# One half of the differential v moved a stage later, and the head norms moved forward, in a decoder block with two attention branches

## The chip, the cores and the metric

The kernel runs on one core of a Trainium2 chip. The core has five engines that work side by side, each with its own queue in a fixed order: TensorE (PE, matmuls and transposes, with weight loads shown as PEld), VectorE (DVE), ScalarE (ACT), GpSimd (POOL) and SyncE (SP), which here issues nearly all loads. Results of matmuls land in PSUM, from where DVE or ACT must move them before the PSUM tile can be used again. The metric is the device time of one launch in microseconds (us); less is better.

## What is computed

The block works on 512 tokens of 1024 channels in float32. Cut to what matters:

```python
xn = rmsnorm(x, norm_mix_g)
q_lat, kv_lat, k_rope, dq, dk, dv, gate_pre = split(xn @ w_in)
# branch A, MLA: 8 heads; q and k from low-rank latents plus a rotary part
o_mla = causal_attention(q_mla, k_mla, v_mla)
# branch B, differential attention: 4 heads, each with two score maps and v of 128 columns
o1 = causal_attention(dq[..., 0, :], dk[..., 0, :], dv)
o2 = causal_attention(dq[..., 1, :], dk[..., 1, :], dv)
o_diff = rmsnorm(o1 - lam * o2, diff_subln_g) * (1 - lambda_init)
gates = sigmoid(gate_pre + b_gate)                     # 2 x 1024 channels
x = x + (g_mla * (o_mla @ w_branch_mla) + g_diff * (o_diff @ w_branch_diff)) @ w_out
x = x + (silu(hn @ w_ffn_gate) * (hn @ w_ffn_up)) @ w_ffn_down     # hn = rmsnorm(x)
return rmsnorm(x, norm_final_g)
```

Causal means that a query block of 128 tokens looks at itself and the blocks before it.

## The kernel before

**Precision.** Every float32 operand of a projection is kept as a pair of rounded halves, high and low (`split`, line 242; `weights`, line 267, for what is loaded), and each product is three matmuls: high by high, high by low, low by high (`mm3`, lines 298 to 300). For a loaded weight tile the high half is made on ACT (L260) and the low half on DVE (L265), 1024 elements a row.

**Tiles.** Buffers come from pools with a fixed number of tiles for each tag (`BUFS`, line 39): 22 "L" tiles of 1024 words a row (q, k, v, pairs of gates, outputs of heads), 5 "t" temporaries of 512, 4 "raw" and 3 "w" tiles for loaded weights and their halves, 6 "P" for probabilities. In PSUM there are 3 "mm" tiles for projections, 2 "sc" for scores, 2 "tr" for transposes and the norm's sums, 1 "pv" for values.

**Order.** The program is traced once, and a scheduler then sets the order of each engine's queue by priorities and its own picture of time: a lower number goes first among what is ready. Three classes are used (lines 124 to 141). `feed` (from 1000 on) is ahead of all: roundings of weights that are used whole, the first two steps of a rotation (L557, L558) and the draining of gates (L480). `attention`, entered with `urgent()`, starts at 100000: the heads. All else has the number of its place in the program, from 1000000 on: this is the fill, projections that are to keep PE busy while a head waits for its softmax.

**Stages.** The fill lists (lines 46 to 54) say which projection is traced ahead of which head. `FILL_MLA` has one entry for each of the four pairs of MLA heads, `FILL_DIFF` one for each differential head. Their items are: `mqk` (q and k of a pair of MLA heads), `mr` (their rotary rows, copied by DMA), `pe` and `mv` (rotary part and v of MLA), `qk` h (q and k of a differential head), `v` c (v of the differential heads 2c and 2c + 1), `gate` b, m (gate of branch b, channels 128m on). A gate, and each of q and k, is 24 matmuls of 512 columns into one "mm" tile with one loaded weight tile. A `v` is 96 matmuls of 256 columns into two "mm" tiles with two loaded weight tiles. Two neighbouring gates (m even and m + 1) share one "L" tile; the even one asks for it (lines 476 to 478). Each half of `v` is drained by four splits into an "L" tile of its own (lines 601 to 605), and q and k of a head take three "L" tiles (line 580) after a rotation in two "t" tiles each (line 555).

**A differential head** (`diff_head`, line 673): for each of four query blocks two maps of scores (L626), on DVE the masked copy with the row maximum (L630), on ACT the exponential (L158), on DVE the reciprocal (L633), then both maps joined (L679 on ACT, L680 on DVE). Then P is transposed on PE (L652) and split (L245, L249), multiplied with v (L663), and the result is copied to a "t" tile (L686) and squared into another (L687). The squares are split into an "L" tile (L690 on DVE, L691 on POOL).

**The norm of a head** (`diff_norm`, line 694): two matmuls with ones sum the squares over the channels into a "tr" tile (L698), then Ln and Exp on ACT, three steps on DVE (L702, L703, L705), one on POOL (L704), and a split into an "L" tile of its own (line 706; L247 on ACT, L251 on DVE). In the loop over the heads (lines 811 to 819) the norm of head h − 1 is traced inside the fill of head h, behind the first item of its list and at the fill's priority; that of the last head is urgent.

After the heads come the 16 sigmoids, the MLA branch (line 825), the differential branch, the output projection, and the FFN.

Of the kernel before, what the change touches and what calls it, by code (L numbers as in the profile page):

```python
# [2 lines left out]

# [1 line left out]

# [16 lines left out]
P = 128  # L22
S = 512
D = 1024
KD = D // P
# [10 lines left out]
OFF = (0, 512, 896, 1152)  # L36
MAGIC = 12582912.0
TWO_PI = 6.283185
BUFS = dict(X=2, L=22, P=6, PT=1, raw=4, w=3, t=5, sm=24)
LAST = 256  # L40
N_WARM = 10
P_DVE = (0, 1)
# [2 lines left out]
W_ENG_BRANCH = ['dve', 'dve']  # L45
FILL = [[("pe", 0), ("mr", 0), ("gate", 0, 2), ("mv", 0)]]
FILL_MLA = [[("mqk", 1), ("mr", 1), ("v", 0), ("pe", 1)],
            [("mqk", 2), ("mr", 2), ("v", 1), ("mv", 1)],
            [("mqk", 3), ("mr", 3), ("qk", 0)],
            [("qk", 1)]]  # L50
FILL_DIFF = [[("qk", 2), ("gate", 0, 3)],
             [("qk", 3), ("gate", 0, 4), ("gate", 0, 5)],
             [("gate", 0, 6), ("gate", 0, 7), ("gate", 1, 0)],
             [("gate", 1, m) for m in range(1, KD)]]
PBUFS = dict(mm=3, sc=2, tr=2, pv=1)


# [31 lines left out]
def build(ctx, nc, tc, a, out):  # L89
# [5 lines left out]
    def nm(s):  # L95
        uid[0] += 1
        return f"{s}_{uid[0]}"

    def T(tag, shape, dtype):
        return sb.tile(shape, dtype, name=nm(tag), tag=tag, bufs=BUFS[tag])  # L100

# [3 lines left out]
    def L_():  # L105
        return T("L", [P, 2, S], F32R)
# [4 lines left out]
    def tmp():  # L111
        return T("t", [P, S], F32)
# [7 lines left out]
    def dma(o, i):  # L120
        nc.sync.dma_start(out=o, in_=i)
# [14 lines left out]
            tc.cur_priority = self.saved  # L136

    attention, feed = Ahead(100000), Ahead(1000)

    def urgent():  # L140
        return attention
# [115 lines left out]
    def round_hi(o, i):  # L257
        if w_eng[0] == 'act':
            with tc.issue_after(hi_last.ins):
                nc.scalar.activation(out=o, in_=i, func=AF.Copy)  # L260
        else:
            nc.vector.tensor_copy(out=o, in_=i)
# [4 lines left out]
    def weights(src, n0, n1, pick=None):  # L267


        raw = T("raw", [P, 1024], F32)  # L270
        n = n0 * n1
        rv = raw[:, :n].rearrange("p (a b) -> p a b", a=n0)
        if isinstance(src, list):
            for i, s_ in enumerate(src):
                dma(rv[:, i, :].rearrange("p (h d) -> p h d", h=s_.shape[1]), s_)
        else:
            dma(rv, src)
        w = T("w", [P, 2, 1024], F32R)
        if pick is None:
            with feed:  # L280
                round_hi(w[:, 0, :n], raw[:, :n])
                round_lo(w[:, 1, :n], raw[:, :n], w[:, 0, :n])
        else:
            nk = sum(h * (d1 - d0) for h, d0, d1 in pick)
            wv = [w[:, s, :n0 * nk].rearrange("p (a b) -> p a b", a=n0) for s in range(2)]
            c = 0
            for h, d0, d1 in pick:
                src_ = rv.rearrange("p a (h e) -> p a h e", h=h)[:, :, :, d0:d1]
                hi, lo = [v[:, :, c:c + h * (d1 - d0)].rearrange("p a (h e) -> p a h e", h=h) for v in wv]
                c += h * (d1 - d0)  # L290
                round_hi(hi, src_)
                round_lo(lo, src_, hi)
            n = n0 * nk
        return [w[:, i, :n].rearrange("p (a b) -> p a b", a=n0) for i in range(2)]
# [196 lines left out]
    qk = {}  # L491

    def fill(work):
        for kind, *args in work:
            if kind == "gate":
                gate(*args)
            elif kind == "v":
                diff_v(*args)
            elif kind == "qk":
                qk[args[0]] = diff_qk(*args)  # L500
            elif kind == "pe":
                pe[args[0]] = mla_pe(*args)
            elif kind == "mv":
                mv[args[0]] = mla_v(*args)
            elif kind == "mqk":
                mqk[args[0]] = mla_qk(*args)
            elif kind == "mr":
                mla_rope(args[0], mqk[args[0]], pe[args[0] // 2])
# [164 lines left out]
    def diff_head(h, products):  # L673
        blocks = []
        for i, p1 in enumerate(prob_tiles()):
            p2 = T("P", [P, S], F32)[:, :(i + 1) * P]
            r1, r2 = scores(list(zip(products, (p1, p2))), i)
            nc.vector.tensor_mul(out=r2, in0=r2, in1=neg_lam)
            nc.scalar.activation(out=p2, in_=p2, func=AF.Copy, scale=r2)  # L679
            nc.vector.scalar_tensor_tensor(out=p1, in0=p1, scalar=r1, in1=p2, op0=ALU.mult, op1=ALU.add)  # L680
            blocks.append(p1)
        pt = transposed(blocks)
        ps = values(pt, lambda j, s: dv[(h // 2) * 2 + j // 2][:, s, (j % 2) * 256 + (h % 2) * P:
                                                              (j % 2) * 256 + (h % 2) * P + P])
        o32, sq = tmp(), tmp()
        nc.scalar.activation(out=o32, in_=ps, func=AF.Copy)  # L686
        nc.scalar.activation(out=sq, in_=ps, func=AF.Square)  # L687
        sqs = L_()
        sqs = [sqs[:, 0, :], sqs[:, 1, :]]
        nc.vector.tensor_copy(out=sqs[0], in_=sq)  # L690
        nc.gpsimd.tensor_sub(out=sqs[1], in0=sq, in1=r32(sqs[0]))  # L691
        return o32, sqs

    def diff_norm(o32, sqs):

        ps = PS("tr")
        for s in range(2):
            nc.tensor.matmul(out=ps, lhsT=ones_r, rhs=sqs[s], start=s == 0, stop=s == 1)  # L698
        y, u = tmp(), tmp()
        log_exp(out=y, in_=ps, func=AF.Ln, scale=1.0 / P, bias=eps)  # L700
        last_exp[0] = log_exp(out=y, in_=y, func=AF.Exp, scale=-0.5)
        nc.vector.scalar_tensor_tensor(out=u, in0=ps, scalar=P * EPS, in1=y, op0=ALU.add, op1=ALU.mult)  # L702
        nc.vector.scalar_tensor_tensor(out=u, in0=u, scalar=-0.5 / P, in1=y, op0=ALU.mult, op1=ALU.mult)  # L703
        nc.gpsimd.tensor_mul(out=o32, in0=o32, in1=y)  # L704
        nc.vector.scalar_tensor_tensor(out=u, in0=u, scalar=1.5, in1=o32, op0=ALU.add, op1=ALU.mult)  # L705
        o = L_()
        split(u, o[:, 0, :], o[:, 1, :], col(R_SG))
        return o

# [85 lines left out]
    mqk, pe, mv = {}, {}, {}  # L795
# [5 lines left out]
    for p in range(4):  # L801
        o = L_()
# [6 lines left out]

    o_diff, parts = [], []  # L810
    for h in range(4):
        fill(FILL_DIFF[h][:1])
        if h > 0:
            o_diff.append(diff_norm(*parts[h - 1]))
        fill(FILL_DIFF[h][1:])
        with urgent():
            parts.append(diff_head(h, qk[h]))
    with urgent():
        o_diff.append(diff_norm(*parts[3]))
# [19 lines left out]
    for c in range(8):  # L839
        half, kp = c // 4, c % 4  # L840
        raw = T("raw", [P, 1024], F32)
        dma(raw.rearrange("p (a b) -> p a b", a=2), kview("w_out", half * S, S, 2 * kp, 2))
        w = None
        if c < 3:
            w = T("w", [P, 2, 1024], F32R)
        elif c == 3:
            w = T("PT", [P, 2, 1280], F32R)
# [36 lines left out]
    for f, n in products[:3]:  # L884
        w = weights(kview(n, f * P, P), KD, P)
# [5 lines left out]
    for n_, (f, n) in enumerate(products):  # L891
        if n_ < 3:
            ps, w = early[n_]
            ffn_product(ps, w, 256, 512)
        else:
            w = weights(kview(n, f * P, P), KD, P)
# [50 lines left out]
    for half in range(2):  # L947
# [8 lines left out]
        for k0 in range(0, NF, 2):  # L956
            w = weights(kview("w_ffn_down", half * S, S, k0, 2), 2, S)
# [42 lines left out]
```

## Time and profile before

| | |
|---|---|
| median of 3 runs | 749.19 us (749.06 to 750.64) |
| the profiled execution | 749.08 us, of it the span of the profile 747.3 us |
| MLA heads, first score matmul to the first differential one | about 74 to 159 us |
| differential heads, first score matmul to the last value matmul | about 159 to 278 us |
| MLA branch begins | 289 us |

The profile is one execution taken by the hardware profiler; times in it run from the start of its span. PE's matmuls are pipelined and their ends are modelled, so PE's busy time holds some overlap; a window in which it is below its full length has real idle time. The views that are used are the page (busy times, the chain that ended last), the windows (busy time and count of each engine in a stretch, also for one line alone), the timeline (instructions in order, with the idle time ahead of them and what ended it in brackets) and groups by line.

### The profile page before, as it was taken

What the parts mean: (1) busy time and instruction counts of PE and PEld (TensorE: products, weight loads), DVE (VectorE), ACT (ScalarE), POOL (GpSimd) and SP (SyncE); (2) the same over time, 40 slices, a digit from 0 to 9 for tenths busy, and PEclk for the clock granted to TensorE, in tenths of its full rate; (3) what the DMA queues carried; (4) which work ended last, traced back from release to release, by engine and by line L of the source; (5) the groups of instructions that cost most, each with busy time, mean ns of one, the idle gap of its engine ahead of it and who ended that gap; (6) DMA issues with size and microseconds to landing.
All of it is one profiled execution on the core that took longest, in us unless ns stands there. A gap on an engine that the chain in (4) does not pass through costs nothing.

```text
span 747.3 us, 9538 instructions
## 1 busy us (share of the span) xinstructions
PE 731.1 (98%) x3602; PEld 618.2 (83%) x3602; DVE 416.9 (56%) x812; ACT 332.5 (44%) x613; POOL 49.9 (7%) x45
## 2 busy tenths in 40 slices
PE   9998999999989989999999999999999999999996
PEld 7977999888868878888898888888888888888885
DVE  7787798988897765695544333342333332122424
ACT  7764788767665633643414232222323222122314
POOL 1000000321240101000000000000000000000302
PEclk9999999999999999999999999999999999999999
DMA  9615344523432312339114333323233232323202
GB/s 336 197 50 137 102 116 100 134 65 97 113 85 63 107 57 85 113 114 281 29 56 114 99 98 89 110 84 113 84 102 96 87 110 86 112 86 109 89 1 112
DMA packets 100414, 78.82 MB, mean 105 GB/s; under 512 B 6416, under 2 KB 87056, under 8 KB 100368
## 3 DMA queue, kind: packets, MB, share of 16 engines
q1 hardware_dynamic: 100080, 78.13, 35.5%
q8 instruction: 28, 0.46, 0.3%
q14 instruction: 18, 0.15, 0.1%
q10 hardware_dynamic: 288, 0.08, 0.0%
HBM read 71.91 MB, written 2.10 MB: 99 GB/s over the span
## 4 chain that ended last, share of the span: by engine, by line
PE 68%; DVE 6%; ACT 2%; issue 1%; DMA 0%; DVEq 0%; ACTq 0%
PE ps_mm L298 19%; PE ps_mm L299 19%; PE ps_mm L300 19%; DVE w L265 2%; PE ps_sc L298 1%; PE ps_sc L300 1%; PE ps_tr L300 1%; PE ps_tr L298 1%; PE ps_tr L299 1%; PE ps_sc L299 1%; DVE P L630 1%; PE ps_pv L300 1%; PE ps_pv L298 1%; PE ps_pv L299 1%; DVE L L249 1%
## 5 line engine op out<-in xcount | busy, mean ns | idle before, releaser
L265 DVE TENSOR_TENSOR w<-raw,w 128x1024 fp32r<-128x1024 f32 (+3 forms) x114 | 136.1, 1196 | 160.7 <-ACT w L260 160.0
L260 ACT ACTIVATE w<-raw 128x1024 fp32r<-128x1024 f32 (+3 forms) x110 | 109.5, 998 | 254.3 <-issue 154.6
L298 PE MATMUL ps_mm<-X,w 128*128 128x512 f32 (+1 forms) x568 | 217.8, 384 | 4.7 <-DVE t L558 4.6
L299 PE MATMUL ps_mm<-X,w 128*128 128x512 f32 (+1 forms) x568 | 217.7, 383 | 0.0
L300 PE MATMUL ps_mm<-X,w 128*128 128x512 f32 (+1 forms) x568 | 217.3, 383 | 0.0
L298 PEld LDWEIGHTS ps_mm<-X,w 128*128 128x128 f32 x568 | 107.1, 189 | 26.0 <-issue 2.8
L299 PEld LDWEIGHTS ps_mm<-X,w 128*128 128x128 f32 x568 | 107.3, 189 | 20.0 <-issue 0.2
L300 PEld LDWEIGHTS ps_mm<-X,w 128*128 128x128 f32 x568 | 107.2, 189 | 20.0
L905 DVE TENSOR_TENSOR t<-t,ps_mm 128x512 f32<-128x512 f32 x22 | 15.1, 688 | 66.4 <-PE ps_mm L300 65.7
L158 ACT ACTIVATE P<-P,sm 128x128 f32<-128x128 f32 (+3 forms) x64 | 35.7, 558 | 25.6 <-DVE sm L630 25.2
L931 POOL TENSOR_TENSOR L<-L,P 128x512 f32<-128x512 f32 (+1 forms) x9 | 12.6, 1414 | 436.2 <-ACT t L930 436.2
L626 PE MATMUL ps_sc<-L,L 96*128 96x128 f32 (+7 forms) x160 | 36.6, 324 | 1.2 <-DVE sm L630 1.2
L299 PE MATMUL ps_mm<-w,L 128*128 128x512 f32 (+1 forms) x100 | 37.2, 372 | 0.0
L298 PE MATMUL ps_mm<-w,L 128*128 128x512 f32 (+1 forms) x100 | 37.1, 373 | 0.0
L300 PE MATMUL ps_mm<-w,L 128*128 128x512 f32 (+1 forms) x100 | 37.0, 373 | 0.0
L299 PE MATMUL ps_mm<-L,w 128*128 128x512 f32 x90 | 35.4, 394 | 0.0
L298 PE MATMUL ps_mm<-L,w 128*128 128x512 f32 x90 | 35.2, 393 | 0.0
L300 PE MATMUL ps_mm<-L,w 128*128 128x512 f32 x90 | 35.2, 391 | 0.0
L245 ACT ACTIVATE L<-t 64x512 fp32r<-64x512 f32 (+2 forms) x47 | 29.2, 621 | 10.2 <-DVE t L779 3.7
L630 DVE CUSTOM_DVE_ANT_0 P<-ps_sc,mask 128x128 f32<-128x128 f32 (+3 forms) x64 | 30.6, 477 | 3.5 <-PE ps_sc L626 3.3
L626 PEld LDWEIGHTS ps_sc<-L,L 96*128 96x128 f32 (+1 forms) x160 | 27.1, 189 | 4.9 <-DVE sm L630 1.7
L249 DVE TENSOR_TENSOR L<-t,L 128x512 fp32r<-128x512 f32 (+2 forms) x37 | 27.7, 749 | 3.6 <-ACT L L245 3.1
(271 smaller groups left out, 1136.6 us busy)
## 6 DMA issues: line engine op xcount, KB each, us to landing
raw<-w_in SPq DMA_DIRECT2D x28, 512.0 KB, 4.5
raw<-w_ffn_gate SPq DMA_DIRECT2D x22, 512.0 KB, 3.9
raw<-w_ffn_up SPq DMA_DIRECT2D x22, 512.0 KB, 3.9
raw<-w_ffn_down SPq DMA_DIRECT2D x22, 512.0 KB, 3.6
L<-x SPq DMA_DIRECT2D x8, 512.0 KB, 7.4
L<-L SPq DMA_DIRECT2D x32, 128.0 KB, 3.4
raw<-w_out SPq DMA_DIRECT2D x8, 512.0 KB, 3.8
L<-xt SPq DMA_DIRECT2D x8, 256.0 KB, 4.3
```

The source lines that it names most:

```text
L158: return nc.scalar.activation(**kw)
L245: nc.scalar.activation(out=hi, in_=src, func=AF.Copy, scale=scale)
L249: nc.vector.tensor_sub(out=lo, in0=src, in1=r32(hi))
L260: nc.scalar.activation(out=o, in_=i, func=AF.Copy)
L265: (nc.vector if w_eng[1] == 'dve' else nc.gpsimd).tensor_sub(out=o, in0=i, in1=r32(hi))
L298: nc.tensor.matmul(out=o, lhsT=lh, rhs=rh, start=start, stop=False)
L299: nc.tensor.matmul(out=o, lhsT=lh, rhs=rl, start=False, stop=False)
L300: return nc.tensor.matmul(out=o, lhsT=ll, rhs=rh, start=False, stop=stop)
L626: nc.tensor.matmul(out=ps[:, :n], lhsT=q[:, i * P:n], rhs=k[:, 0:n], start=j == 0, stop=j == last)
L630: nc.vector.tensor_tensor_reduce(out=m, in0=ps[:, :n], in1=mask[:, S - n:], scale=-1.0, scalar=3.4e38, op0=ALU.add, op1=ALU.min, accum_out ...
L905: nc.vector.tensor_mul(out=g, in0=g, in1=ps)
L931: nc.gpsimd.tensor_mul(out=xs, in0=xs, in1=g)
```

## The change

Five things are edited. There is a sixth "t" temporary. The second half of the differential v (`v` 1) moves from the second MLA entry to the first differential entry; the gates (0,3) and (0,4) take its place, and the gates behind them each move forward, so that the last entry has six gates instead of seven. The weight roundings that had `feed` priority keep it only from the differential stage on; before, they have the priority of their place in the program. The norm writes its result into the "L" tile that held the squares, instead of into a new one. And the norm of head h − 1 is traced after all of the fill of head h, inside `urgent()`, just ahead of head h.

```diff
-BUFS = dict(X=2, L=22, P=6, PT=1, raw=4, w=3, t=5, sm=24)
+BUFS = dict(X=2, L=22, P=6, PT=1, raw=4, w=3, t=6, sm=24)
...
 FILL_MLA = [[("mqk", 1), ("mr", 1), ("v", 0), ("pe", 1)],
-            [("mqk", 2), ("mr", 2), ("v", 1), ("mv", 1)],
+            [("mqk", 2), ("mr", 2), ("gate", 0, 3), ("gate", 0, 4), ("mv", 1)],
             [("mqk", 3), ("mr", 3), ("qk", 0)],
             [("qk", 1)]]
-FILL_DIFF = [[("qk", 2), ("gate", 0, 3)],
-             [("qk", 3), ("gate", 0, 4), ("gate", 0, 5)],
-             [("gate", 0, 6), ("gate", 0, 7), ("gate", 1, 0)],
-             [("gate", 1, m) for m in range(1, KD)]]
+FILL_DIFF = [[("qk", 2), ("v", 1)],
+             [("qk", 3), ("gate", 0, 5), ("gate", 0, 6)],
+             [("gate", 0, 7), ("gate", 1, 0), ("gate", 1, 1)],
+             [("gate", 1, m) for m in range(2, KD)]]
...
     attention, feed = Ahead(100000), Ahead(1000)
+    parts_first = [False]
...
         if pick is None:
-            with feed:
+            with feed if parts_first[0] else nullcontext():
                 round_hi(w[:, 0, :n], raw[:, :n])
                 round_lo(w[:, 1, :n], raw[:, :n], w[:, 0, :n])
...
-        sqs = L_()
-        sqs = [sqs[:, 0, :], sqs[:, 1, :]]
+        o = L_()
+        sqs = [o[:, 0, :], o[:, 1, :]]
         nc.vector.tensor_copy(out=sqs[0], in_=sq)
         nc.gpsimd.tensor_sub(out=sqs[1], in0=sq, in1=r32(sqs[0]))
-        return o32, sqs
-
-    def diff_norm(o32, sqs):
+        return o32, sqs, o
+
+    def diff_norm(o32, sqs, o):
...
-        o = L_()
         split(u, o[:, 0, :], o[:, 1, :], col(R_SG))
         return o
...
     for h in range(4):
-        fill(FILL_DIFF[h][:1])
-        if h > 0:
-            o_diff.append(diff_norm(*parts[h - 1]))
-        fill(FILL_DIFF[h][1:])
+        parts_first[0] = True
+        fill(FILL_DIFF[h])
         with urgent():
+            if h > 0:
+                o_diff.append(diff_norm(*parts[h - 1]))
             parts.append(diff_head(h, qk[h]))
```

More of the change, by code (lines that the diff above doesn't have):

```diff
@@ L1 @@
 import math
-from contextlib import ExitStack
+from contextlib import ExitStack, nullcontext
 import numpy as np
```

## The prediction

> **What bounds the kernel now.** First the page's head, the busy times and the chain that ended last:
>
> ```profile
> span 747.3 us, 9538 instructions
> PE 731.1 (98%) x3602; PEld 618.2 (83%) x3602; DVE 416.9 (56%) x812; ACT 332.5 (44%) x613; POOL 49.9 (7%) x45
> PE 68%; DVE 6%; ACT 2%; issue 1%; DMA 0%; DVEq 0%; ACTq 0%
> ```
>
> TensorE (PE) is the bound: whatever keeps it from a matmul adds to the time, and no change of order can bring more than its idle time. The change leaves every matmul in place, so only idle time counts. Next, the windows of the attention stages:
>
> ```profile
> 70.00:130.00 60.00, 60.00 (x423) 56.35 (x422) 50.07 (x137) 48.09 (x108) 0.00 (x0) 1.00 0.44 114
> 130.00:184.00 54.00, 54.00 (x283) 46.12 (x281) 48.76 (x112) 38.67 (x80) 11.82 (x8) 1.00 0.42 103
> 203.00:208.70 5.70, 3.12 (x18) 2.20 (x17) 4.87 (x15) 4.21 (x9) 0.49 (x1) 1.00 0.38 93
> 221.60:224.90 3.30, 2.09 (x13) 1.45 (x11) 3.27 (x13) 2.67 (x6) 0.00 (x0) 1.00 0.01 1
> 267.30:271.70 4.40, 2.47 (x14) 1.40 (x11) 4.26 (x7) 2.54 (x4) 0.77 (x1) 1.00 0.00 1
> 280.00:290.00 10.00, 10.00 (x46) 8.26 (x45) 3.54 (x6) 0.00 (x0) 2.14 (x1) 1.00 0.35 105
> ```
>
> Columns: the stretch, its length, then busy time and count of PE, weight loads, VectorE (DVE), ScalarE (ACT) and POOL, the clock, DMA. From 70 to 184 us, which is all of MLA and the start of head 0, PE never idles. In the differential stage it idles in three places: 5.70 − 3.12 = 2.58, 3.30 − 2.09 = 1.21 and 4.40 − 2.47 = 1.93, **5.72 us together**. That is the prize. From 280 us on PE is full again.
>
> Why does PE idle there, with projections left to do? Call the 24 matmuls of 512 columns that fill one "mm" PSUM tile a product; 8 of them are on L300. The windows of L300 alone count products:
>
> ```profile
> 184.10:203.30 19.20, 9.47 (x24) 4.51 (x24) 1.00 0.39 91
> 203.30:208.60 5.30, 0.00 (x0) 0.00 (x0) 1.00 0.34 83
> 208.60:221.70 13.10, 6.26 (x16) 3.00 (x16) 1.00 0.45 115
> 221.70:224.90 3.20, 0.00 (x0) 0.00 (x0) 1.00 0.01 1
> 224.90:267.50 42.60, 18.86 (x48) 9.03 (x48) 1.00 0.31 87
> 267.50:271.60 4.10, 0.00 (x0) 0.00 (x0) 1.00 0.00 0
> ```
>
> Three products, none, two, none, six, none. By the order of the fill lists, the three before 203.3 are q and k of head 3 and gate (0,4); the two are gates (0,5) and (0,6). "mm" has three PSUM tiles, and fill stops when all three are full and undrained. Who drains them, and when?
>
> ```profile
> 206.54 0.58 ACT L686 ACTIVATE t<-ps_pv 128x512 f32<-128x512 f32 x1
> 207.02 0.59 ACT L687 ACTIVATE t<-ps_pv 128x512 f32<-128x512 f32 x1
> 207.35 0.72 DVE L557 STREAM_SHUFFLE t<-ps_mm 128x512 f32<-128x512 f32 x1
> 207.96 0.67 DVE L558 TENSOR_TENSOR t<-ps_mm,tab 128x512 f32<-128x512 f32 x1
> 208.69 0.50 PE L298 MATMUL ps_mm<-X,w 128*128 128x512 f32 x1 [2.21 <-DVE t L558]
> 223.78 0.72 ACT L247 ACTIVATE L<-t,cols 128x512 fp32r<-128x512 f32 x1
> 224.20 1.28 DVE L480 TENSOR_TENSOR L<-ps_mm,x_rms 128x512 f32<-128x512 f32 x2
> 269.45 0.72 ACT L247 ACTIVATE L<-t,cols 128x512 fp32r<-128x512 f32 x1 [0.29 <-DVE t L705]
> 270.94 1.88 DVE L480 TENSOR_TENSOR L<-ps_mm,x_rms 128x512 f32<-128x512 f32 x3
> ```
>
> The rotation of head 3's q (L557, L558) comes only behind the two temporaries of head 0 (L686, L687), although it has the highest priority and its product is long done. Gates (0,4) and (0,5) are drained together (L480 x2) only behind the first write of norm 0's output tile (L247, 223.78); three more wait for that of norm 2 (269.45). Each time, the one that waits stands in the program after the one that goes first, and both want a tile of the same tag ("t", "L"). I read this as: tiles of one tag are handed out in the program's order, whatever the priority. This reading carries the forecast.
>
> **The change part by part.** *Norms in the squares' tile, and urgent.* Two more rows, the first writes of the square tiles of heads 0 and 2:
>
> ```profile
> 209.79 1.24 DVE L690 CAST L<-t 128x512 fp32r<-128x512 f32 x1
> 258.77 0.43 DVE L690 CAST L<-t 128x512 fp32r<-128x512 f32 x1 [0.61 <-DMA raw<-w_branch_mla]
> ```
>
> The norm takes no "L" tile any more, so no gate stands behind it. Gate (0,4) gets its tile in the MLA stage and (0,5) shares it; (0,6) stands behind head 0's square tile, written at 209.79, long before 221. So the idle at 221.6 goes: −1.21. Later, gates (1,2) and (1,3) stand behind head 2's square tile, 258.77, instead of norm 2's output, 269.45: 10.7 us sooner. So a PSUM tile is free when the V matmuls of head 3 wait at 268 for transposed P, and fill covers that wait: −1.93. What then is late is head 3 itself, whose last matmuls run beside three more gates and the MLA branch; at 280–290 PE is at its full pace, 46 matmuls in 10 us, 0.217 us each, 5.2 us a product, so three products cover 15.6 us of head 3's latency. The norm's instructions (two matmuls, three ACT, four DVE, one POOL a head) are the same in number; they now go ahead of the next head's softmax on DVE, four times some 0.7 us. That costs nothing on PE while fill has a PSUM tile, and would be paid as up to 2.8 us a head if it had none. The write into the squares' tile adds no wait: the norm's matmuls have read it before the Ln that the write depends on.
>
> *Second half of v in stage 0, two gates in its place.* Columns are equal: 96 matmuls of 256 against 48 of 512, zero on PE, and two 512 KB loads for two on the one SP queue:
>
> ```profile
> raw<-w_in SPq DMA_DIRECT2D x28, 512.0 KB, 4.5
> 184.00:290.00 106.00, 100.28 (x480) 82.50 (x480) 80.65 (x180) 54.08 (x114) 21.81 (x15) 1.00 0.31 85
> ```
>
> A load lands in 4.5 us, four "raw" tiles run ahead and the DMA engines are busy 0.31 of the stage, so they wait for nothing. ACT gets four more instructions in this stage and DVE 4 × 0.48 (v) − 2 × 0.68 (the drains of the two gates) = 0.56 us; ACT is half idle there (54.08 of 106), DVE a quarter (80.65). What counts is the place: between q/k of head 2 and q/k of head 3 there stand now two PSUM tiles of v instead of one gate. Everything behind moves one product later, so at 206 head 3's q and k hold two PSUM tiles and the third is free for gate (0,5): the idle at 203 goes, −2.58. The sixth temporary helps the second rotation there and is counted at nothing, since PE waited for the first; its cover is that free PSUM tile.
>
> The price is at 182, where the first half of v stands instead of gate (0,3):
>
> ```profile
> 182.76 0.68 DVE L480 TENSOR_TENSOR L<-ps_mm,x_rms 128x512 f32<-128x512 f32 x1
> 184.16 0.48 PE L298 MATMUL ps_mm<-X,w 128*128 128x512 f32 x1
> 184.67 0.67 DVE L558 TENSOR_TENSOR t<-ps_mm,tab 128x512 f32<-128x512 f32 x1
> 195.86 0.69 DVE L249 TENSOR_TENSOR L<-t,L 64x512 fp32r<-64x512 f32 x1
> L251 DVE SCALAR_TENSOR_TENSOR L<-ps_mm,sm,L x8: 478/480/484, 82.4 to 123.9; 128x256 fp32r<-128x256 f32 x8
> ```
>
> Gate (0,3) is drained at once, as its tile is there already, and PE goes on at 184.16. A half of v needs an "L" tile that stands behind the three of head 2's q and k, and its drain (two ACT, two DVE of 0.48) has no high priority. So all three PSUM tiles are held, and behind the next product on PE's queue the whole fill waits, until the first rotation ends at 184.67 + 0.67 = 185.34: **+1.18**. Bounds: 0 if attention fills the time, and above, the first rival.
>
> *Rounding behind attention until the differential stage.*
>
> ```profile
> L265 DVE TENSOR_TENSOR w<-raw,w 128x1024 fp32r<-128x1024 f32 x10 | 13.9, 1390 | 2.0 <-ACT w L260 1.8
> 55.16 1.23 DVE L265 TENSOR_TENSOR w<-raw,w 128x1024 fp32r<-128x1024 f32 x1 [0.20 <-ACT w L260]
> 60.20 0.47 PE L298 MATMUL ps_mm<-X,w 128*128 128x512 f32 x1 [2.38 <-DVE t L558]
> 60.30:64.50 4.20, 4.20 (x13) 3.25 (x14) 4.14 (x8) 1.23 (x2) 0.00 (x0) 0.62 0.40 111
> 184.13 0.60 ACT L778 ACTIVATE t<-ps_pv 64x512 f32<-64x512 f32 x1
> 188.46 0.67 DVE L779 TENSOR_TENSOR t<-ps_pv,t 64x512 f32<-64x512 f32 x1
> ```
>
> Of the ten roundings between 60 and 160 us, eight lose their place ahead of attention (two of v, two gates, four of q and k). With three "w" tiles a rounding is made two products before its use. At 19.2 / 3 = 6.4 us a product (attention included), that covers 12.8 us, while the longest DVE delay I find behind other work is L779's, 188.46 − 184.73 = 3.73 us. So: 0 on PE. Below zero: the wait at 57–60 us comes out of a full DVE, and the rounding at 55.16 stands ahead of the rotation; behind it, up to 1.23 us and the slow clock after it, 4.2 × (1 − 0.62) = 1.60 us, could go. I take 0, as at 55.16 nothing else was ready.
>
> Sum: −2.58 − 1.21 − 1.93 + 1.18 = **−4.54 us**. The profiled execution took 749.08 us (1.8 us beside its span), next to the median of 749.19: 749.08 − 4.54 = **744.5 us**.
>
> **The rivals.**
>
> *The half of v blocks longer.* After 185.34 the two rotated PSUM tiles carry PE for two products, 12.8 us, to 198.1. The drain of v must come after head 2's k is split, 195.86 + 0.69 = 196.55, plus its own four halves of 0.48: 198.5, just even. Behind attention by L779's 3.73 us it is 202.2: PE idles 4.1 us, and by the stretch after 60.20 the clock falls too, 1.6. 744.5 + 5.7 = 750.2. For it: the drain's low priority; against it: DVE had waits of its own around 197.
>
> *Fill starves in MLA.* If a rounding waits over the 12.8 us of cover, PE idles for the excess at each of eight tiles. At 1 us of excess: +8, so 752.5, slower than before. For it: DVE is busy 50.07 of 60 us from 70 on, and attention now goes first; nothing in that stretch has idle time to give back. Against it: the q, k and v splits have stood behind attention all along and PE never idled. It decides at a delay of 12.8 us, 3.4 times the 3.73.
>
> *Also the wait at 57 goes*: −1.23 − 1.60, 741.7. The Trainium skill (TensorE: Matmul & The Clock Gate, the HAM clock gate) has the clock fall only after an idle window of about 3.4 us. By that rule the 2.38 us at 60.20 would not be the cause of the slow stretch, only the 1.23 would be won, and this case would be at 743.3. The trace speaks against the rule here: 0.62 right behind 2.38 us of waiting; yet after the 2.21 us at 208.69 the clock stayed at 1.00.
>
> *Nothing changes*: were tiles not handed out in program order, the drains were late for another reason, DVE's own queue (4.87 busy of 5.70 us at 203), and would stay late: 749.1.
>
> **How the numbers follow.** The forecast 0.58; the wait at 57 also gone 0.09; v blocks 0.10; nothing 0.07; starved fill 0.16. The measurement can tell about 0.2%, 1.5 us. Faster: 0.58 + 0.09 = 0.67; within: 0.10 + 0.07 = 0.17; slower 0.16. The range goes from the fast case at 741.7, a little less, to 750.9, just over the case in which v blocks; starved fill is left out.
>
> **What would show it.** Right: L480 follows within about 1 us of its product's last matmul at all gates; no window without L300 between 200 and 275; norm matmuls (L698) straight behind L691; PE's wait for L558 near 207 gone, and a wait of about 1 us near 184. Wrong: L480 again in pairs; a wait of PE behind L249/L251 of v near 198; any PE idle between 70 and 184, with L265 or L260 as the releaser, which would be starved fill; a different gap at the end of head 3, before the sigmoids.

## The result, and the profile after

| | before | after |
|---|---|---|
| median | 749.16 us (749.06 to 750.64) | 740.32 us (740.15 to 740.50) |
| ratio, with its 95% interval | | 0.9877 (0.9862 to 0.9891) |
| profiled execution, its span | 749.08, 747.3 us | 740.23, 738.5 us |
| first MLA score matmul | 73.65 us | 69.69 us |
| MLA branch begins | 289.02 us | 280.16 us |
| from there to the end of the span | 458.3 us | 458.3 us |

The change is faster by 8.84 us. The forecast was 744.5, so the sign was right and the size half of what came; the time lies below the range, which began a little under 741.7. The table says already where: 3.96 us are gained before the first MLA score, 4.90 more by the start of the MLA branch, nothing after it. The forecast of −4.54 concerned the second part alone. One execution of a kernel further below (tile and rounding) ran at a granted clock of 0.655 and took 1043.41 us; its ratio leaves it out.

In the changed kernel lines 139 to 705 have a number higher by one (L298 is now L299). Its page, the head and the chain that ended last:

```profile
span 738.5 us, 9543 instructions
PE 729.0 (99%) x3602; PEld 617.2 (84%) x3602; DVE 413.6 (56%) x812; ACT 333.7 (45%) x613; POOL 48.4 (7%) x45
PE 96%; DVE 3%; ACT 0%; issue 0%; DVEq 0%
```

PE has as many matmuls as before (x3602). Before, 68% of the last chain were PE's and 6% DVE's; now it is 96% and 3%: hardly anything is waited for. The windows of the changed kernel, the stretches of the prediction and two more (57 to 61 and 179 to 185.5), columns as there:

```profile
57.00:61.00 4.00, 4.00 (x19) 3.07 (x18) 3.96 (x9) 1.01 (x2) 0.00 (x0) 1.00 0.76 179
60.30:64.50 4.20, 4.20 (x25) 3.69 (x24) 4.17 (x8) 1.21 (x3) 0.00 (x0) 1.00 0.64 155
70.00:130.00 60.00, 60.00 (x372) 53.93 (x372) 49.57 (x137) 45.66 (x103) 0.00 (x0) 1.00 0.52 129
179.00:185.50 6.50, 5.46 (x42) 5.07 (x42) 6.43 (x17) 3.94 (x9) 4.76 (x4) 1.00 0.00 0
203.00:208.70 5.70, 5.70 (x31) 4.91 (x30) 5.35 (x13) 2.99 (x7) 1.50 (x2) 1.00 0.38 92
221.60:224.90 3.30, 3.30 (x18) 2.76 (x17) 3.30 (x9) 1.82 (x5) 1.29 (x1) 1.00 0.66 159
267.30:271.70 4.40, 4.40 (x24) 3.62 (x23) 3.71 (x6) 1.49 (x3) 0.00 (x0) 1.00 0.06 13
```

The three idle places of the differential stage are full (5.70 of 5.70, 3.30 of 3.30, 4.40 of 4.40). Two are new: 6.50 − 5.46 = 1.04 us between 179 and 185.5, and 0.27 us in two short waits near 195. And the stretch from 57 to 61 is full too, at clock 1.00 in what follows. In the kernel before, that window reads:

```profile
57.00:61.00 4.00, 1.62 (x9) 1.04 (x8) 3.94 (x9) 1.60 (x3) 0.00 (x0) 1.00 0.84 214
```

2.38 us of it were idle, and 4.2 us at clock 0.62 followed. The longer part of the new wait, in the list of waits of PE, and the one pair among the ten drains of gates between 160 and 280 us, in the timeline behind the row ahead of it:

```profile
PE ps_mm L299 <- DVE t L559: 0.9, 1, 0.9
```

```profile
256.63 0.43 DVE L691 CAST L<-t 128x512 fp32r<-128x512 f32 x1 [0.95 <-ACT t L688]
256.98 1.28 DVE L481 TENSOR_TENSOR L<-ps_mm,x_rms 128x512 f32<-128x512 f32 x2
```

The wait is the foretold one, for the end of a rotation (L559), once, with 0.86 us; the other 0.18 of the 1.04 are scores that wait for VectorE. And of the gates, which went in twos and threes (1.28 and 1.88 us), eight are now drained singly; two go together at 256.98, behind the write of head 2's square tile (L691), where the prediction put gates (1,2) and (1,3), and PE does not idle there.

A first balance by idle time: −2.38 (at 57) − 1.60 (slow clock behind it) − 5.72 + 1.04 + 0.27 = −8.39 of 8.84. It comes near, but a balance made from the result proves no cause, and five edits are in it. Each is taken apart below.

### The profile page after: what moved, and what is told of

Its sections match the earlier page's. It is cut to its first block, busy times and chain, and to the rows that moved or that the text cites. A ratio compares the mean times of both kernels' runs of the same rounds, so it can differ in the third digit from the quotient of the medians.

```text
span 738.5 us, 9543 instructions
## 1 busy us (share of the span) xinstructions
PE 729.0 (99%) x3602; PEld 617.2 (84%) x3602; DVE 413.6 (56%) x812; ACT 333.7 (45%) x613; POOL 48.4 (7%) x45
## 4 chain that ended last, share of the span: by engine, by line
PE 96%; DVE 3%; ACT 0%; issue 0%; DVEq 0%
PE ps_mm L299 25%; PE ps_mm L300 25%; PE ps_mm L301 25%; PE ps_sc L627 3%; PE ps_tr L653 2%; PE ps_tr L301 2%; PE ps_sc L300 2%; PE ps_sc L299 2%; PE ps_sc L301 2%; PE ps_tr L299 2%; PE ps_tr L300 2%; PE ps_pv L774 1%; PE ps_pv L664 1%; PE ps_pv L301 1%; PE ps_pv L300 1%; PE ps_pv L299 1%
## 5 line engine op out<-in xcount | busy, mean ns | idle before, releaser
L266 DVE TENSOR_TENSOR w<-raw,w 128x1024 fp32r<-128x1024 f32 (+3 forms) x114 | 133.7, 1175 | 159.8 <-ACT w L261 159.5
L299 PE MATMUL ps_mm<-X,w 128*128 128x512 f32 (+1 forms) x568 | 217.3, 383 | 0.1
L299 PEld LDWEIGHTS ps_mm<-X,w 128*128 128x128 f32 x568 | 106.7, 188 | 20.4 <-issue 0.3
L299 PE MATMUL ps_mm<-w,L 128*128 128x512 f32 (+1 forms) x100 | 37.1, 373 | 0.0
L299 PE MATMUL ps_mm<-L,w 128*128 128x512 f32 x90 | 35.4, 395 | 0.0
```

Of the source, the lines that this page charges most:

```text
L266: (nc.vector if w_eng[1] == 'dve' else nc.gpsimd).tensor_sub(out=o, in0=i, in1=r32(hi))
L299: nc.tensor.matmul(out=o, lhsT=lh, rhs=rh, start=start, stop=False)
```

## The experiments

Each time is a median, its ratio to the kernel before measured on the same chip; the medians of before were 749.13, 749.84 and 749.15 in the three groups. "Alone" means the kernel before with this edit only. Theory A throughout: tiles of one tag are handed out in the program's order, which makes the waits in the differential stage; the wait at 57 is one of priorities.

| kernel | median, us | ratio (95%) | first MLA score, us | MLA branch begins, us | between, us |
| --- | --- | --- | --- | --- | --- |
| rounding alone | 746.99 | 0.9971 (0.9958 to 0.9985) | 70.00 | 288.74 | 218.74 |
| sixth temporary alone | 747.37 | 0.9960 (0.9944 to 0.9975) | 73.31 | 287.31 | 214.00 |
| norm in the squares' tile alone | 744.33 | 0.9923 (0.9908 to 0.9937) | 73.45 | 284.33 | 210.88 |
| fill lists alone | 743.40 | 0.9911 (0.9893 to 0.9929) | 73.75 | 284.41 | 210.66 |
| one weight's rounding alone | 745.86 | 0.9944 (0.9923 to 0.9964) | 70.39 | 286.36 | 215.97 |
| change without the rounding part | 744.19 | 0.9924 (0.9901 to 0.9946) | 71.92 | 282.60 | 210.68 |
| tile and rounding | 742.70 | 0.9907 (0.9883 to 0.9932) | 69.59 | 282.14 | 212.55 |
| lists and rounding | 740.19 | 0.9881 (0.9866 to 0.9896) | 69.59 | 280.04 | 210.45 |
| change with five temporaries | 740.21 | 0.9882 (0.9866 to 0.9899) | 69.58 | 279.95 | 210.37 |
| change with late norms | 740.09 | 0.9879 (0.9864 to 0.9894) | 69.69 | 280.10 | 210.41 |
| change with v first | 738.88 | 0.9858 (0.9838 to 0.9879) | 69.64 | 277.43 | 207.79 |
| that, and sigmoids first | 737.62 | 0.9845 (0.9831 to 0.9860) | 70.18 | 276.32 | 206.14 |

"Between" is from the first MLA score to the begin of the MLA branch, with the same work of PE in it in all rows but the last (there a part of head 3 comes after that point); it is 215.37 us in the kernel before and 210.47 in the changed one. These three columns are from the profiled execution of each kernel.

### The norm's tile alone

```diff
-        sqs = L_()
-        sqs = [sqs[:, 0, :], sqs[:, 1, :]]
+        o = L_()
+        sqs = [o[:, 0, :], o[:, 1, :]]
...
-        return o32, sqs
+        return o32, sqs, o
...
-    def diff_norm(o32, sqs):
+    def diff_norm(o32, sqs, o):
...
-        o = L_()
         split(u, o[:, 0, :], o[:, 1, :], col(R_SG))
```

> Before plus one part: the norm writes its result into the tile of the squares; its place in the program and its priority stay. Theory A (the gates stood behind the norm's output tile in the program's order): the idle places at 221 (1.21) and 268 us (1.93) go, the one at 203 (2.58) and the wait at 57 stay: 749.1 - 3.1 = 746.0 us, and L480 follows its product within about 1 us at gates (0,4) to (1,1). Rival B (DVE's own queue or the norm's low priority made the drains late): L480 still comes in pairs behind the norm, 749 us.

Windows of this kernel, then two of the drains of gates in its timeline, and last a row of the kernel before:

```profile
57.00:61.00 4.00, 1.63 (x6) 1.01 (x5) 3.94 (x9) 1.44 (x3) 0.00 (x0) 0.88 0.85 239
185.50:208.70 23.20, 20.62 (x101) 16.93 (x100) 20.81 (x50) 14.24 (x31) 5.94 (x5) 1.00 0.41 97
220.00:225.00 5.00, 5.00 (x28) 4.32 (x27) 4.91 (x15) 2.46 (x6) 0.05 (x1) 1.00 0.42 104
266.00:272.00 6.00, 6.00 (x31) 5.00 (x31) 4.35 (x8) 2.23 (x4) 0.00 (x0) 1.00 0.30 90
```

```profile
216.48 1.28 DVE L480 TENSOR_TENSOR L<-ps_mm,x_rms 128x512 f32<-128x512 f32 x2
266.17 0.68 DVE L480 TENSOR_TENSOR L<-ps_mm,x_rms 128x512 f32<-128x512 f32 x1
```

```profile
216.69 0.39 PE L698 MATMUL ps_tr<-L,ones_r 128*128 128x512 f32 x1
```

The first pair goes at 216.48 instead of 224.20, a second one is left at 234.29, all later gates go singly, and the idle time at 221 and 268 is gone; that at 203 to 208 (23.20 − 20.62 = 2.58) and the one at 57 stand as they were. Nothing else was touched than which tile the norm writes to, so it is shown that the gates stood behind the norm's tile. That the order of the program put them there is not shown by this alone, as a mere lack of "L" tiles would be mended by the same edit. The last row speaks for the order: in the kernel before, the last read of head 0's square tile ends at 217.08, yet the pair that wants an "L" tile goes only at 224.20, behind the first write of the norm's. The size is larger than the idle time: between the two points this kernel takes 210.88 us and the kernel before 215.37, 4.49 us less for 1.21 + 1.93 = 3.14 us of idle time. The last section comes back to it.

### The fill lists alone

```diff
-            [("mqk", 2), ("mr", 2), ("v", 1), ("mv", 1)],
+            [("mqk", 2), ("mr", 2), ("gate", 0, 3), ("gate", 0, 4), ("mv", 1)],
...
-FILL_DIFF = [[("qk", 2), ("gate", 0, 3)],
-             [("qk", 3), ("gate", 0, 4), ("gate", 0, 5)],
-             [("gate", 0, 6), ("gate", 0, 7), ("gate", 1, 0)],
-             [("gate", 1, m) for m in range(1, KD)]]
+FILL_DIFF = [[("qk", 2), ("v", 1)],
+             [("qk", 3), ("gate", 0, 5), ("gate", 0, 6)],
+             [("gate", 0, 7), ("gate", 1, 0), ("gate", 1, 1)],
+             [("gate", 1, m) for m in range(2, KD)]]
```

> Before plus one part: the new fill lists (v moved, two gates in its place). Theory A: at 203 a PSUM tile is free, and the idle 2.58 us there goes; near 182 PE waits about 1 us, as a half of v is held; the idle 1.21 at 221 goes too, since gate (0,5) now has its tile early and only (0,6) stands behind norm 0; the one at 268 shrinks, since gate (1,2) is now the first item of the last list and no longer behind norm 2. Together -2.6 - 1.2 + 1.0 - (0 to 1.9): 744.4 to 746.3 us. Rival B (the norm's place alone matters): 203 goes, 221 and 268 stay, 747.5 us. Rival C (the moved v blocks): a wait of 3 us or more between 182 and 200, 750 us.

Windows of this kernel, then rows of its timeline:

```profile
179.00:185.50 6.50, 5.49 (x37) 4.61 (x35) 6.35 (x20) 5.18 (x14) 0.47 (x1) 1.00 0.00 1
185.50:208.70 23.20, 22.92 (x128) 19.54 (x129) 21.10 (x50) 16.05 (x35) 5.20 (x4) 1.00 0.37 91
220.00:225.00 5.00, 5.00 (x24) 4.16 (x23) 4.86 (x12) 4.63 (x11) 0.52 (x1) 1.00 0.54 147
266.00:272.00 6.00, 6.00 (x28) 4.88 (x27) 4.86 (x7) 2.16 (x4) 1.30 (x1) 1.00 0.30 90
```

```profile
227.88 0.71 ACT L247 ACTIVATE L<-t,cols 128x512 fp32r<-128x512 f32 x1
```

```profile
228.10 0.69 DVE L480 TENSOR_TENSOR L<-ps_mm,x_rms 128x512 f32<-128x512 f32 x1
```

The lists bring the new wait (6.50 − 5.49 = 1.01) and take away the idle time at 203 and 221, as theory A had it; that at 268, which was to shrink, is gone as well, and 743.40 lies 1.0 below theory A's range. All this comes without the tile, to which the prediction had given 221 and 268. The rows show that a gate still stands behind the norm's output (228.10 right behind the L247 at 227.88) and later ones still go in pairs (at 249.38, 261.24 and 271.21). I read this as: with the order moved by one product fewer PSUM tiles are held at that time, and PE does not run out; how many were held was not counted. So the tile part and the lists are two cures of one trouble. Each alone brings the branch to 284.3 or 284.4; they don't add.

### Rounding alone, and one weight's rounding alone

```diff
+    parts_first = [False]
...
-            with feed:
+            with feed if parts_first[0] else nullcontext():
...
     for h in range(4):
+        parts_first[0] = True
         fill(FILL_DIFF[h][:1])
```

> Before plus one part of the change: the weight roundings have their high priority only from the differential stage on. Theory A (this part took away the wait of PE at 57 us and the slow clock behind it): PE's wait for L559 near 57 to 60 us is gone and the clock stays at 1.00 there; 749.1 - 2.4 - 1.6 = 745.1 us; the three idle places of the differential stage (2.58, 1.21, 1.93 us) are all still there, some 4 us earlier. Rival B (the sixth temporary or the new fill lists did it): the wait at 57 is unchanged, 749 us. Rival C (rounding behind attention starves the fill in MLA): idle time of PE between 70 and 160 us, time above 749.

The first score comes at 70.00 instead of 73.65, so this part carries the gain of the first stage, and MLA did not starve. But the branch begins at 288.74, hardly before 289.02. Of the 218.74 − 215.37 = 3.37 us given back, about half is a stretch of 3.41 us at half clock in this one execution, which took 748.81 us, 1.82 above the median; the window that shows it:

```profile
266.00:272.00 6.00, 4.50 (x20) 3.29 (x19) 5.84 (x10) 2.86 (x5) 0.28 (x1) 0.83 0.28 87
```

The medians stand at 749.13 − 746.99 = 2.14 us. Theory A is confirmed at 57 and missed the total, which it put at 745.1. It also expected the three idle places of the differential stage to stay: their sum did (5.64 us between the two points, for 5.72), but it now lies in eleven waits of PE instead of six.

Then a single rounding only, that of gate (0,2):

```diff
-            with feed:
+            with nullcontext() if late[0] else feed:
...
-    fill(FILL[0])
+    fill(FILL[0][:2])
+    late[0] = True
+    fill(FILL[0][2:3])
+    late[0] = False
+    fill(FILL[0][3:])
```

> The kernel before, in which the rounding of one loaded weight alone, that of gate (0,2), has the priority of its place instead of the one ahead of attention. Theory A (this one rounding, at 54 to 56 us on ScalarE and VectorE, is what kept the split of the MLA q back, and so the PSUM tile for which TensorE waited): the 2.38 us wait at 57 and the 1.6 us of slow clock behind it go, 4.0 us in the first stage, and the MLA and differential stages stay as they are: 745.1 us. Theory B (the stretch is full whatever the order, or it takes the other roundings as well): the wait stays at 1.5 us or more and the time is within 1 us of 749.1. Theory C (a rounding made that late holds gate (0,2) itself back): the wait moves to gate (0,2), 1 us or more on the line of the high-half matmuls behind 58 us.

ScalarE and VectorE in the kernel before, from 54 us on:

```profile
54.08 1.05 ACT L260 ACTIVATE w<-raw 128x1024 fp32r<-128x1024 f32 x1
55.03 0.58 ACT L245 ACTIVATE L<-ps_mm 64x512 fp32r<-64x512 f32 x1
```

```profile
56.30 0.68 DVE L251 SCALAR_TENSOR_TENSOR L<-ps_mm,L 64x512 fp32r<-64x512 f32 x1
59.38 0.66 DVE L558 TENSOR_TENSOR t<-ps_mm,tab 128x512 f32<-128x512 f32 x1
60.08 0.69 DVE L251 SCALAR_TENSOR_TENSOR L<-ps_mm,L 64x512 fp32r<-64x512 f32 x1
```

and in this kernel:

```profile
53.86 0.58 ACT L246 ACTIVATE L<-ps_mm 64x512 fp32r<-64x512 f32 x1
54.34 1.05 ACT L261 ACTIVATE w<-raw 128x1024 fp32r<-128x1024 f32 x1
```

```profile
54.66 0.67 DVE L252 SCALAR_TENSOR_TENSOR L<-ps_mm,L 64x512 fp32r<-64x512 f32 x1
55.42 1.23 DVE L266 TENSOR_TENSOR w<-raw,w 128x1024 fp32r<-128x1024 f32 x1
56.68 0.69 DVE L252 SCALAR_TENSOR_TENSOR L<-ps_mm,L 64x512 fp32r<-64x512 f32 x1
59.87 0.66 DVE L559 TENSOR_TENSOR t<-ps_mm,tab 128x512 f32<-128x512 f32 x1
```

```profile
57.52 0.47 PE L299 MATMUL ps_mm<-X,w 128*128 128x512 f32 x1
```

```profile
57.00:61.00 4.00, 4.00 (x18) 3.08 (x17) 3.96 (x9) 1.01 (x2) 0.00 (x0) 1.00 0.78 197
220.00:225.00 5.00, 3.37 (x12) 2.34 (x13) 5.00 (x16) 4.19 (x10) 0.58 (x1) 0.80 0.43 105
```

The MLA q is split in two parts of 64 rows, one for each head, each with a high half on ScalarE and a low half on VectorE. Before, ScalarE takes the 1.05 us of the rounding first and the high half of the q's first part (L245) after it, so on VectorE its low half is not ready at 55.16, the rounding of 1.23 us fills the hole, and the second part of the same q falls behind both rotations, to 60.08. Its PSUM tile is then free at 60.77, and PE goes on at 60.20 with the rotated one. In the experiment the q's high half goes first, its two low halves end at 56.68 + 0.69 = 57.37, and PE begins the next product at 57.52: no wait, although the rotation ends even later (60.53 for 60.04). So a single rounding, swapped with one step of 0.58 us, decides over 2.38 us of idle time. That is theory A; the total, 745.86, lies 0.8 above its 745.1, and the stretch behind is 215.97 us for 215.37, where no change was expected. Its idle time has moved there too: 4.64 us, in other places than before, and behind some of it the clock fell again (0.80 over 220 to 225, the second window). Why this rounding moves the waits of the later stage was not followed.

### The change without the rounding part

```diff
-    parts_first = [False]
+    parts_first = [True]
```

> The changed kernel with all roundings of whole weights ahead of attention again, from the first one on: the change minus its rounding part. Theory A (of the 8.8 us, 4.0 come from the rounding of one weight in the first stage, 4.5 from the differential stage, which the other parts bring alone): the wait of 2.4 us at 57 and the slow clock behind it come back, no idle time at 203, 221 and 268: 744.3 us. Theory B (the roundings of the MLA and differential stages carry a part of the differential gain): some of the idle time at 203 to 270 comes back, over 745.5 us. Theory C (the wait at 57 goes by something else in the change, the lists or the sixth temporary): near 740.3 us.

Theory A: 744.19. The windows of 57 to 64.5 us:

```profile
57.00:61.00 4.00, 1.63 (x8) 1.05 (x7) 3.94 (x9) 1.51 (x3) 0.00 (x0) 1.00 0.84 237
60.30:64.50 4.20, 4.20 (x20) 3.44 (x20) 4.14 (x8) 1.23 (x2) 0.00 (x0) 1.00 0.36 95
```

The wait is back and the gain of the differential stage stays. 744.19 − 740.32 = **3.87 us** is what the rounding part is worth in the whole change. In this execution the clock stayed at 1.00 behind the wait; it took 742.69 us, the three others 744.17 to 744.40. That splits the 3.87 into about 2.4 for the wait (742.69 − 740.32) and 1.5 for the slow clock, which follows in most executions, not in all.

### Two parts together

Tile and rounding as in the diffs above, with the old lists:

> The kernel before with two of the parts, the norm's result in the squares' tile and the roundings behind attention until the differential stage; lists, place of the norm and five temporaries as before. Theory A (in the differential stage either the tile or the lists brings all that is to be had there, 4.5 us, and the rounding brings 4.0 in the first stage): 740.3 us, the same as the whole change within 0.5 us. Theory B (with the roundings late the differential stage of the old lists idles anew, as it did with the rounding part alone, where its excess rose by 3.8 us): 743 us or more, with idle time of PE between 186 and 223.

Theory B, as to the place: 742.70, with idle time between 186 and 206.

```profile
185.50:208.70 23.20, 20.27 (x94) 15.48 (x92) 21.98 (x51) 15.04 (x33) 9.26 (x7) 1.00 0.37 91
```

2.93 us are idle there (23.20 − 20.27), in short waits of 0.2 to 0.8, where the tile alone left 2.58 in two. Against the tile alone the stretch between the two points is 212.55 − 210.88 = 1.67 us longer, and by the medians the rounding brings 744.33 − 742.70 = 1.63 us here instead of 3.87. Lists and rounding instead, with the old norm and five temporaries:

> The kernel before with two parts, the new fill lists and the roundings behind attention until the differential stage; tile and place of the norm and five temporaries as before. Theory A (the new lists bring the whole differential gain alone, and it is the old lists alone under which late roundings give 2 to 3 us back between 186 and 206): 740.3 us, as the whole change, with one wait of about 1 us near 180. Theory B (late roundings give 2 us back in the differential stage whatever the lists, and it is the norm's tile or place, or the sixth temporary, that mends it in the whole change): 742.5 us, PE idle between 186 and 206.

```profile
179.00:185.50 6.50, 5.47 (x43) 5.09 (x42) 6.45 (x16) 3.91 (x9) 4.82 (x4) 1.00 0.00 0
185.50:208.70 23.20, 22.93 (x117) 19.01 (x117) 20.80 (x55) 16.29 (x36) 2.42 (x3) 1.00 0.47 114
```

740.19, theory A: lists and rounding are the whole change. Under the new lists late roundings cost nothing (210.45 between the two points, 210.66 with the lists alone); under the old ones they give back about 2 us (3.87 − 1.63 here, 3.87 − 2.14 in the rounding alone). Which wait of theirs comes from which rounding was not taken apart.

### The rest of the change

Five temporaries in the changed kernel, and the sixth alone in the kernel before:

```diff
-BUFS = dict(X=2, L=22, P=6, PT=1, raw=4, w=3, t=6, sm=24)
+BUFS = dict(X=2, L=22, P=6, PT=1, raw=4, w=3, t=5, sm=24)
```

> The changed kernel with five temporaries again. Theory A (the sixth is worth nothing beside the rest, since what PE waited for at 203 is covered by the new lists): 740.3 us within 0.5. Theory B (the second rotation of a head waits for a temporary again and PE with it, as the 1.7 us that the sixth brought alone may mean): 742 us, a wait of 1.5 us or more near 200 for the second step of a rotation.

> Before plus a sixth temporary alone. Theory A (tiles of a tag are handed out in the program's order, so that a rotation waits for its turn and not for a number of tiles; the wait at 57 comes from the roundings): PE's idle places at 57, 203, 221 and 268 us all stay, 749 us within 1. Rival B (temporaries are short): the wait at 57 goes (745.1 us), or the one at 203 goes (746.5 us), or both (742.5 us).

With five it takes 740.21, against 740.32. Alone, the sixth brought 0.4% (0.9960), mostly at 268: the window there

```profile
266.00:272.00 6.00, 5.37 (x28) 4.31 (x27) 5.90 (x10) 2.58 (x5) 1.11 (x1) 1.00 0.05 17
```

has 0.63 us idle instead of 1.93. The waits at 57 and 206 stayed, so the number of temporaries is not what makes them; at 268 theory A, which had all four places stay and 749 us within 1, was wrong. What the sixth does bring, the lists bring already.

The norm's place, with its result still in the squares' tile:

```diff
-        fill(FILL_DIFF[h])
-        with urgent():
-            if h > 0:
-                o_diff.append(diff_norm(*parts[h - 1]))
+        fill(FILL_DIFF[h][:1])
+        if h > 0:
+            o_diff.append(diff_norm(*parts[h - 1]))
+        fill(FILL_DIFF[h][1:])
+        with urgent():
```

> The changed kernel with the norm of a head traced inside the fill again, behind its first item and at the fill's priority, but still with its result in the squares' tile. Theory A (the norm's early place is worth nothing: no gate stands behind its tile any more, and its output is needed in the differential branch only): 740.3 us within 0.5. Theory B (a late norm holds temporaries, and the next head's values behind them): 742 us or more, PE idle on the line of the values or of the high-half matmuls between 215 and 275.

740.09: the early place is worth nothing. One more "L" tile in the kernel before, which would have told a shortage of tiles from their order directly, was not tried.

### A version that is faster than both

What the change leaves is the wait near 180 that it brings in. Two edits after it, one at a time:

```diff
-FILL_DIFF = [[("qk", 2), ("v", 1)],
+FILL_DIFF = [[("v", 1), ("qk", 2)],
```

> The changed kernel with the first differential entry turned round: the second half of v ahead of q and k of head 2. Theory A (the one wait that the change brings in, 1.04 us near 180, comes from v standing between the rotated products, so that all three PSUM tiles are held): ahead of them v finds its tiles free, the wait goes, nothing else changes: 739.3 us. Theory B (v's tiles of the tag L stand behind others there too and the wait only moves): 740.3 us, a wait of about 1 us elsewhere between 165 and 190. Theory C (q of head 2 comes too late for its head): 741 us or more, PE idle ahead of head 2 or at 203.

```diff
-    with urgent():
-        o_diff.append(diff_norm(*parts[3]))
-
-
     sigmoids(last_exp[0], (0, 1))
+    o_diff.append(diff_norm(*parts[3]))
```

> The changed kernel with the second half of v ahead of q and k of head 2, and the norm of the last head traced behind the sigmoids, at the priority of its place. With the first edit alone one wait of 1.03 us is left, at 286, for a product of the MLA branch whose gate has not seen its sigmoid yet. Theory A (the sigmoids wait for the two logarithm and exponential steps of the last norm at 282 to 284): they start near 279, the wait goes: 737.9 us. Theory B (they wait for the last gate or for the table): the wait stays, 738.9 us. Theory C (the last norm comes too late for the differential branch, or a table more is loaded): 739.5 us or more, PE idle behind 320.

With v ahead of q and k of head 2, two windows and three rows:

```profile
179.00:185.50 6.50, 6.50 (x34) 5.52 (x33) 4.68 (x17) 3.44 (x8) 0.00 (x0) 1.00 0.31 81
280.00:290.00 10.00, 8.97 (x40) 7.06 (x39) 6.23 (x9) 7.52 (x11) 1.28 (x1) 1.00 0.34 106
```

```profile
283.79 1.28 ACT L488 ACT_TABLE_LOAD   x1
285.09 4.40 ACT L488 ACTIVATE L<-L,cols 128x512 f32<-128x512 f32 x7
287.27 0.50 PE L299 MATMUL ps_mm<-L,w 128*128 128x512 f32 x1 [1.03 <-DVE L L792]
```

The wait near 180 is gone, and the branch begins 2.7 us sooner, but half of that is lost again: a product of the MLA branch now waits 1.03 us, since the sigmoids of its gate (L488) begin only behind the last norm's Ln and Exp and a table load. With the sigmoids ahead of that norm:

```profile
280.00:290.00 10.00, 10.00 (x49) 8.38 (x48) 6.31 (x8) 2.60 (x4) 1.30 (x1) 1.00 0.35 112
```

That wait goes too: 737.62 us, 2.70 below the change and 1.55% below the kernel before (0.9845). Both times theory A, except that the first edit won 1.44 us, with the wait behind it, where 1.04 was expected; it also ended the 0.27 us near 195.

## Why the prediction was half right

- **Tiles in program order: right, as far as the runs go.** Taking the norm's "L" tile away, and nothing else, ended the waits at 221 and 268; the rows speak for the order rather than for a lack of tiles, which no run tested by itself.
- **The three idle places go (−5.72): right as places, wrong as a sum of parts.** The forecast gave 221 and 268 to the tile and 203 to the lists. The lists remove all three; the tile removes 221 and 268 by itself and leaves 203. The two don't add: 210.66 and 210.88 us between the two points, 210.68 with both (the change without the rounding part).
- **The new wait (+1.18): right in place and cause,** 0.86 us for a rotation, 1.04 with the scores next to it. In time it is dearer: with v first the stretch between the two points is 210.47 − 207.79 = 2.68 us shorter, for 1.31 us of idle time.
- **The sum −4.54: confirmed, in part by compensation.** The change without its rounding part takes 744.19 (forecast 744.5). But the idle places cost more than their idle time (4.49 for 3.14 at 221 and 268) and the new wait did too (2.68 for 1.31); the two errors are of opposite sign, and that they cancel is luck. So "no change of order can bring more than its idle time" was wrong: from the kernel before to the one with v first the stretch is 215.37 − 207.79 = 7.58 us shorter, for 5.72 of idle time.
- **Norms urgent, and the sixth temporary, at 0: right.** 740.09 without the one, 740.21 without the other.
- **Rounding behind attention, "So: 0 on PE ... I take 0, as at 55.16 nothing else was ready": this is the step that failed.** It measured −3.87 us, nearly all of the miss of 4.2. The row at 55.16 was read on VectorE alone. Nothing else was ready there because ScalarE had done the high half of the same weight's rounding first, at 54.08, ahead of the q split that VectorE would have continued. Both halves are moved by the same edit, so the moment has to be replayed from ScalarE's queue on.
- **The rival "also the wait at 57 goes" (741.7, a chance of 0.09) named the place and undersized it.** It gave back the 1.23 us of the rounding out of 2.38, as if PE would still wait for the same rotation. PE took another PSUM tile, q's, so the whole wait went. With 2.38 for 1.23 the rival would have been at 740.5. The slow clock was priced right, 1.60.
- **Fill starves in MLA: did not happen.** PE is busy 60.00 of 60.00 us from 70 on, with attention ahead of the roundings. The v halves did not block longer either: no wait behind their splits is left in the list.

The cover of 12.8 us for late roundings was thus right under the new lists only. Under the old ones the same edit gives back about 2 us between 186 and 206, which the forecast did not see.

## What to carry to other kernels

When an edit lets an instruction lose its place, replay every engine on which it has a half, from the earliest one, and ask which buffer comes free first then; the wait that the page names may be replaced by a different release, not shortened by the length of the moved step. Where several parts aim at neighbouring waits of one engine, price them together: each may be enough, and their gains then don't add. A wait by order of tiles is cured by needing no tile as well as by moving the order, and the first left the rest of the schedule as it was.

## What the runs showed of the hardware

**A wait costs more than the idle time shown.** In the experiment with the norm's tile, 3.14 us of idle time gone gave 4.49 us. A part of it can be read off the rows: a matmul is shown longer than the distance to the next one. In the changed kernel's timeline

```profile
58.21 0.39 PE L301 MATMUL ps_mm<-X,w 128*128 128x512 f32 x1
58.43 0.40 PE L299 MATMUL ps_mm<-X,w 128*128 128x512 f32 x1
```

the second starts 0.22 us after the first, which is shown as 0.39. The next matmul can be late by 0.17 us before any idle time appears, so each wait hides that much, and shorter ones don't appear at all. The four gaps at 221 and 268 hide 0.7 us so; where the rest of the 1.35 lies was not taken apart.

**The clock fell behind a wait of 2.38 us, in some executions.** Behind the same wait, the profiled execution of before ran at clock 0.62 from 60.3 to 64.5 us, and that of the change without rounding at 1.00, faster by 1.5 to 1.7 us than the other executions of the same kernel. The kernel before shows the same steps, with executions near 747.4, 749.1 and 750.6 us; of these only one near 749.1 was profiled.

The traces show more. In their clock records every stretch at half speed begins a whole number of times 3.41 us after the record's first entry, and each one that is over before the span ends is 3.41 us long. The number is 16 (54.61 us) in the kernel before and in those with the sixth temporary, the tile or the lists alone, 64 (218.45) with one weight's rounding and 77 (262.83) with the rounding part alone. So the clock is set window by window. Here are two windows of this grid in the kernel before, where the first entry stands at 6.70 us, and two in the change without rounding, where it stands at 3.84:

```profile
57.90:61.31 3.41, 1.11 (x5) 0.97 (x6) 3.35 (x7) 0.96 (x2) 0.00 (x0) 1.00 0.90 259
61.31:64.72 3.41, 3.41 (x10) 2.63 (x9) 3.38 (x7) 1.23 (x2) 0.00 (x0) 0.50 0.29 64
```

```profile
55.04:58.45 3.41, 2.67 (x14) 1.81 (x12) 3.38 (x6) 2.40 (x5) 0.00 (x0) 1.00 0.28 54
58.45:61.86 3.41, 1.78 (x8) 1.52 (x9) 3.35 (x7) 0.76 (x2) 0.00 (x0) 1.00 0.79 253
```

Before, one window holds 3.41 − 1.11 = 2.30 us of idle time, and the next runs at 0.50. Without the rounding part the grid cuts the same wait into 0.74 and 1.63 us, and the clock stays. The falls with the rounding part alone and with one weight's rounding came behind windows with 1.50 and 1.41 us of idle time, while with the tile alone 1.72 us (206.80 to 210.21) were followed by none; so these runs give no sharp bound. A wait of this length thus costs 2.4 us and, where the grid lies badly, about 1.6 more; the changed kernel, without it, keeps within 740.15 to 740.50. The Trainium skill (TensorE: Matmul & The Clock Gate, The HAM clock gate) has a free-running window of about 3.4 us, and the records agree with their 3.41. The Trainium skill's table of states there asks for a whole idle window, and the first row, with PE busy for 1.11 us of it, speaks against that.
